# Three DMAs of 112, 8 and 8 partitions in place of one of 128, in the tail of a row sum

## The chip, the cores and the metric

The kernel runs on one core of one Trainium2 chip. The metric is the device time of one execution in microseconds (us). Before the change the median of three runs is 160.55 us (160.5 to 160.6). The profile is of a further execution, which took 160.47 us.

## What is computed

Each of 32 x 512 rows of 1024 float32 numbers is summed and the sum multiplied by 0.5.

```python
def setup_inputs():
    batch, seq, dim = 32, 512, 1024
    return {
        "x": np.random.randn(batch, seq, dim).astype(np.float32),
        "multiplier": 0.5,
    }

def reference(x: np.ndarray, multiplier: float) -> np.ndarray:
    return (np.sum(x, axis=-1) * multiplier).astype(np.float32)
```

## The kernel before

The 16384 rows are 128 for each of 128 partitions. One row per partition is the "head"; it is loaded first (L112), summed by ACT and turned into a form for its own small store by DVE (L113 to L119). The other 127 rows per partition are loaded in eight blocks: one of 15 rows, six of 16, and a last one of 16 that is loaded in five pieces. Three buffers (`xb`) of 16 rows go round. A row is 4 KB, so a block of 16 rows is 8 MB.

All DMAs are issued by SP, in the order of the program, and share one queue, whose transfers are served in order on the 16 DMA engines. The helper `load` (L79 to L88) allocates a semaphore, issues one `dma_start` (L82), which may wait first for a count of DVE's finished instructions (`free`, the buffer is free again) or for another load to land (`behind`), and adds 16 to the semaphore when all of it has landed. Whatever stands behind a waiting issue on SP waits too.

For the first six blocks DVE sums the whole block (L136) and scales the sums (L142). The seventh block is shared: DVE sums eight of its rows, ACT the other eight (`act_row`, L91). The last block comes in these pieces, which are named here for the rest of the text:

- p0: rows 0 to 9; p1: rows 10 to 13; p2: row 14 and the first 384 columns of row 15 (L163 to L173, sizes in `bounds`);
- e0: columns 384 to 735 of row 15, 352 columns, 1408 B per partition; e1: the last 288 columns (L174 to L182, sizes in `cuts`).

e0 and e1 go to a tensor `end` of their own. e0 is issued when the seventh block has landed (`behind`), e1 when DVE has summed its half of the seventh block (`free`).

In the last block ACT sums rows 1, 4, 7, 9, 13 and 14 and DVE the others, each as a sum of two halves with an accumulator (`dve_sum`, L101; in the profile a CUSTOM_DVE_ANT_0 and a READ_ACCUMULATOR). Row 15 is summed in three steps on DVE: the first 384 columns as 192 pairs (L205), e0's 352 columns as 176 pairs (L207, `second`), and e1's 288 columns together with the two partial sums, as 145 pairs (L210, `final`). `second` waits for e0 (L206). `final` waits for 17 on e1's semaphore: 16 of its landing and one that `second` adds (L209, L211).

There are three stores. The results of the first seven blocks go out after ACT's and DVE's parts of the seventh block (L184, "the early store"). The head's results follow in a DMA of four partitions of 128 B each (L188). The last store (L214) waits for 2 on `summed_up`: one from ACT after row 14 (L200) and one from `final` (L212). SP then waits for all stores.

Of the kernel before, what the change touches and what calls it, by code (L numbers as in the profile page):

```python
# [9 lines left out]
def kernel(  # L10
# [13 lines left out]
    nc = tc.nc  # L24
# [4 lines left out]
    P = nc.NUM_PARTITIONS  # L29
# [4 lines left out]
    N, D = x_flat.shape  # L34
# [4 lines left out]
    B = 16  # L39
    n_blocks = rows // B  # L40
# [5 lines left out]
    x_last = x_flat[P * own : N, :].rearrange("(p c) d -> p c d", p=P)  # L46
# [4 lines left out]
    def sbuf(name, *shape):  # L51
        return ctx.enter_context(nc.sbuf_tensor(name, list(shape), fp32)).ap()
# [8 lines left out]
    cuts = [384, 736, D]  # L61
    at = 368
    end = sbuf("end", P, at + D - cuts[1])

    def sem(name):
        return nc.alloc_semaphore(name=name)

    dve_done = sem("dve_done")
# [7 lines left out]
        counts[engine] += 1  # L76
        return counts[engine]

    def load(name, dst, src, free=None, behind=None):  # L79

        landed = sem(name)
        i = nc.sync.dma_start(out=dst, in_=src)  # L82
        if free is not None:
            i.wait_op(dve_done, free, "sem-ge")
        if behind is not None:
            i.wait_op(behind, 16, "sem-ge")
        i.then_inc(landed, 16)
        return landed  # L88

    def act_row(t, r, dst):  # L90
        return nc.scalar.activation(  # L91
            out=t[:, r, :],
            in_=t[:, r, :],
            func=mybir.ActivationFunctionType.Copy,
            scale=mul,
            accum_out=dst,
        )

    def dve_sum(row, dst, scale):
        mid = row.shape[-1] // 2  # L100
        return nc.vector.tensor_tensor_reduce(  # L101
            out=row[:, 0:mid],
            in0=row[:, 0:mid],
            in1=row[:, mid:],
            scale=scale,
            scalar=0.0,
            op0=ADD,
            op1=ADD,
            accum_out=dst,
        )  # L110

    landed_head = load("landed_head", head[:, 0, :], x_flat[0:P, :])  # L112
    cleared = marks(nc.vector.memset(column, 0.0), "dve")  # L113
    nc.scalar.wait_ge(landed_head, 16)
# [6 lines left out]
    freed = []  # L121
    blocks = []
    for b, n in enumerate(sizes):
        c0 = 1 + sum(sizes[:b])
        t = buf[b % bufs][:, 0:n, :]
        landed = load(
            f"landed{b}",
            t,
            x_rows[:, c0 - 1 : c0 - 1 + n, :],
            freed[b - bufs] if b >= bufs else None,  # L130
        )
# [5 lines left out]
                out=sums[:, c0 : c0 + h], in_=t[:, 0:h, :], axis=mybir.AxisListType.X  # L137
# [5 lines left out]
            out=res[:, c0 : c0 + h],  # L143
            in_=sums[:, c0 : c0 + h],
# [5 lines left out]
        if h < n:  # L150
            nc.scalar.wait_ge(landed, 16)
            for r in range(h, n):
                i = act_row(t, r, res[:, c0 + r : c0 + r + 1])
# [5 lines left out]
    flat = t.rearrange("p c d -> p (c d)")  # L159
    flat_last = x_last.rearrange("p c d -> p (c d)")  # L160
    bounds = [0, 10 * D, 14 * D, 15 * D + cuts[0]]

    landed = [  # L163
        load(f"landed_p{k}", flat[:, lo:hi], flat_last[:, lo:hi], free, behind)
        for k, (lo, hi, free, behind) in enumerate(
            zip(
                bounds[:-1],
                bounds[1:],
                (None, None, freed[n_blocks - 3]),
                (None, blocks[n_blocks - 3], None),  # L170
            )
        )
    ]  # L173
    landed_end = [  # L174
        load(f"landed_e{k}", end[:, to : to + hi - lo], x_last[:, B - 1, lo:hi], free, behind)
        for k, (to, lo, hi, free, behind) in enumerate(
            (
                (0, cuts[0], cuts[1], None, blocks[n_blocks - 2]),
                (at, cuts[1], D, freed[n_blocks - 2], None),
            )  # L180
        )
    ]  # L182
# [10 lines left out]
    on_act = {1, 4, 7, 9, 13, 14}  # L193
    for k, (lo, hi) in enumerate(((0, 10), (10, 14), (14, 15))):
        on = [r for r in range(lo, hi) if r in on_act]
        nc.scalar.wait_ge(landed[k], 16)
        for r in on:
            i = act_row(t, r, res[:, c0 + r : c0 + r + 1])
        if k == len(landed) - 1:
            i.then_inc(summed_up, 1)  # L200
        on = [r for r in range(lo, hi) if r not in on_act]
        nc.vector.wait_ge(landed[k], 16)
        for r in on:
            dve_sum(t[:, r, :], res[:, c0 + r : c0 + r + 1], mul)
    dve_sum(t[:, B - 1, 0 : cuts[0]], end[:, at - 2 : at - 1], 1.0)  # L205
    nc.vector.wait_ge(landed_end[0], 16)  # L206
    second = dve_sum(end[:, 0 : cuts[1] - cuts[0]], end[:, at - 1 : at], 1.0)  # L207

    second.then_inc(landed_end[1], 1)  # L209
# [75 lines left out]
```

## Time and profile before

| what | value |
|---|---|
| median of 3 runs | 160.55 us (160.5 to 160.6) |
| the profiled execution | 160.47 us |
| its span (first to last profiled event) | 159.2 us |
| DMA queue, share of 16 engines' span | 98.0% |
| HBM read | 67.11 MB, 422 GB/s over the span |
| e0: from issue to landing | 19.2 us |
| e1: from issue to landing | 10.8 us |
| last store: from issue to landing | 1.4 us |

The span is what the profile covers; 1.3 us of the execution's time lie around it. All times inside the execution are from the span's start. "To landing" is from the issue of a DMA on SP to the last increment of its semaphore; a DMA that is issued behind others in the queue spends most of this time waiting for them. The profile's page groups instructions by line, engine and shape; the timeline lists them in order of time, with the idle time before each in square brackets and what ended it. The trace also records every increment of a DMA's semaphore and every packet of a transfer, with its start, duration and size, but not which of the 16 DMA engines carried it.

### The profile page before, as it was taken

How to read it: one execution, taken by the hardware profiler on the slowest of the kernel's cores; microseconds unless marked ns; L12 is line 12 of the kernel's file. 1: busy time of each engine (PE TensorE's matmuls, PEld its weight loads, DVE VectorE, ACT ScalarE, POOL GpSimd, SP SyncE). 2: the span in 40 equal slices, each digit the busy share in tenths (PEclk: the TensorE clock that was granted, in tenths of full speed). 3: DMA queues.
4: the chain of work that ended last, by engine and by line, in shares of the span. 5: the costliest groups of instructions: out<-in, count | busy, mean ns of one | idle time of the engine just before them, and what ended most of it. 6: DMA issues, size and time to landing. Idle time of an engine off the chain costs nothing.

```text
span 159.2 us, 131 instructions
## 1 busy us (share of the span) xinstructions
DVE 119.1 (75%) x40; ACT 17.4 (11%) x31; POOL 0.2 (0%) x4
## 2 busy tenths in 40 slices
DVE  0000059995799968999599995999959999598376
ACT  2300000000000000000000000000000000397384
POOL 0000000000000000000000000000000000000000
DMA  9997996996997999969969969969989799798994
GB/s 379 494 401 340 494 527 264 527 527 264 527 461 329 527 395 395 527 280 511 527 264 527 527 264 527 494 296 527 445 346 527 346 445 527 329 453 371 420 401 151
DMA packets 2168, 67.18 MB, mean 422 GB/s; under 512 B 504, under 2 KB 760, under 8 KB 1016
## 3 DMA queue, kind: packets, MB, share of 16 engines
q1 hardware_dynamic: 2168, 67.18, 98.0%
HBM read 67.11 MB, written 0.07 MB: 422 GB/s over the span
## 4 chain that ended last, share of the span: by engine, by line
DMA 74%; DVE 24%; another core or an unknown queue 1%; SPq 1%; issue 0%
DMA xb<-in_x_dram 74%; DVE sums L136 22%; DVE xb L101 1%; SPq L82 1%; DVE end L101 0%; DVE res L142 0%; DVE res L101 0%
## 5 line engine op out<-in xcount | busy, mean ns | idle before, releaser
L136 DVE TENSOR_REDUCE sums<-xb 128x16 f32<-128x16384 f32 (+2 forms) x7 | 110.9, 15849 | 28.4 <-DMA xb<-in_x_dram 28.4
L91 ACT ACTIVATE xb<-xb 128x1024 f32<-128x1024 f32 x14 | 14.6, 1045 | 137.1 <-DMA xb<-in_x_dram 137.1
L101 DVE CUSTOM_DVE_ANT_0 xb<-xb 128x512 f32<-128x512 f32 (+1 forms) x10 | 5.9, 652 | 4.4 <-DMA xb<-in_x_dram 4.4
L91 ACT ACTIVATION_READ_ACCUMULATOR xb<-xb 128x1 f32 x14 | 2.6, 187 | 0.0
L113 DVE MEMSET column<- 128x32 f32 x1 | 0.1, 85 | 3.0 <-PEq L26 3.0
L117 DVE STREAM_TRANSPOSE row<-column 128x32 f32<-128x32 f32 x1 | 0.2, 212 | 2.6 <-ACT head L91 2.6
L91 ACT ACT_TABLE_LOAD x1 | 1.3, 1283 | 3.1 <-DVE column L113 3.1
L142 DVE TENSOR_SCALAR res<-sums 128x16 f32<-128x16 f32 (+2 forms) x7 | 1.2, 174 | 0.2
L91 ACT ACTIVATE head<-head 128x1024 f32<-128x1024 f32 x1 | 1.1, 1056 | 0.0
L101 DVE DVE_READ_ACCUMULATOR2_ANT res<- 128x1 f32 x10 | 0.8, 80 | 0.0
L101 DVE CUSTOM_DVE_ANT_0 end<-end 128x176 f32<-128x176 f32 (+1 forms) x2 | 0.7, 326 | 0.0
L91 ACT ACTIVATION_READ_ACCUMULATOR head<-head 128x1 f32 x1 | 0.2, 186 | 0.0
L101 DVE DVE_READ_ACCUMULATOR2_ANT end<- 128x1 f32 x2 | 0.2, 82 | 0.0
L266 POOL MEMSET const-bfloat16-1.0<- 128x1 bf16 x1 | 0.1, 101 | 0.0
L266 POOL MEMSET const-uint8-127<- 128x1 uint8 x1 | 0.1, 101 | 0.0
L266 POOL MEMSET const-float32-0.0<- 128x1 f32 x1 | 0.1, 98 | 0.2 <-issue 0.2
L266 POOL MEMSET const-float32-1.0<- 128x1 f32 x1 | 0.1, 98 | 0.0
## 6 DMA issues: line engine op xcount, KB each, us to landing
xb<-in_x_dram SPq DMA_DIRECT2D x1, 7680.0 KB, 21.2
xb<-in_x_dram SPq DMA_DIRECT2D x1, 5120.0 KB, 33.6
xb<-in_x_dram SPq DMA_DIRECT2D x1, 2048.0 KB, 36.4
xb<-in_x_dram SPq DMA_DIRECT2D x1, 704.0 KB, 20.8
head<-in_x_dram SPq DMA_DIRECT2D x1, 512.0 KB, 3.3
end<-in_x_dram SPq DMA_DIRECT2D x1, 176.0 KB, 19.2
end<-in_x_dram SPq DMA_DIRECT2D x1, 144.0 KB, 10.8
xb<-in_x_dram SPq DMA_DIRECT2D x6, 40.8
```

Source lines behind the costliest of these rows:

```text
L82: i = nc.sync.dma_start(out=dst, in_=src)
L91: return nc.scalar.activation(out=t[:, r, :], in_=t[:, r, :], func=mybir.ActivationFunctionType.Copy, scale=mul, accum_out=dst,)
L101: return nc.vector.tensor_tensor_reduce(out=row[:, 0:mid], in0=row[:, 0:mid], in1=row[:, mid:], scale=scale, scalar=0.0, op0=ADD, op1=ADD, ...
L113: cleared = marks(nc.vector.memset(column, 0.0), "dve")
L117: turned = nc.vector.transpose(out=row, in_=column)
L136: nc.vector.reduce_sum(out=sums[:, c0 : c0 + h], in_=t[:, 0:h, :], axis=mybir.AxisListType.X),
L142: scaled = nc.vector.tensor_single_scalar(out=res[:, c0 : c0 + h], in_=sums[:, c0 : c0 + h], scalar=mul, op=mybir.AluOpType.mult,)
L266: nc = _bacc.Bacc("TRN2", target_bir_lowering=False, num_devices=1)
```

## The change

`load` takes a list of partition counts and issues one DMA for each, all on the same semaphore; only the first one waits. The wait for e0 then asks for 16 times the number of DMAs. Only e0 gets more than one: 112, 8 and 8 partitions. The sums, the columns and the other loads stay as they are.

```diff
-    def load(name, dst, src, free=None, behind=None):
+    def load(name, dst, src, free=None, behind=None, groups=(P,)):
 
         landed = sem(name)
-        i = nc.sync.dma_start(out=dst, in_=src)
-        if free is not None:
-            i.wait_op(dve_done, free, "sem-ge")
-        if behind is not None:
-            i.wait_op(behind, 16, "sem-ge")
-        i.then_inc(landed, 16)
+        p0 = 0
+        for n in groups:
+            i = nc.sync.dma_start(out=dst[p0 : p0 + n], in_=src[p0 : p0 + n])
+            if free is not None and p0 == 0:
+                i.wait_op(dve_done, free, "sem-ge")
+            if behind is not None and p0 == 0:
+                i.wait_op(behind, 16, "sem-ge")
+            i.then_inc(landed, 16)
+            p0 += n
+        assert p0 == P
         return landed
...
+    groups_end = (112, 8, 8)
     landed_end = [
...
-                (0, cuts[0], cuts[1], None, blocks[n_blocks - 2]),
-                (at, cuts[1], D, freed[n_blocks - 2], None),
+                (0, cuts[0], cuts[1], None, blocks[n_blocks - 2], groups_end),
+                (at, cuts[1], D, freed[n_blocks - 2], None, (P,)),
...
-    nc.vector.wait_ge(landed_end[0], 16)
+    nc.vector.wait_ge(landed_end[0], 16 * len(groups_end))
```

More of the change, by code (lines that the diff above doesn't have):

```diff
@@ L161 @@
     bounds = [0, 10 * D, 14 * D, 15 * D + cuts[0]]
+    groups = ((P,), (P,), (P,))
     landed = [
-        load(f"landed_p{k}", flat[:, lo:hi], flat_last[:, lo:hi], free, behind)
-        for k, (lo, hi, free, behind) in enumerate(
+        load(f"landed_p{k}", flat[:, lo:hi], flat_last[:, lo:hi], free, behind, parts)
+        for k, (lo, hi, free, behind, parts) in enumerate(
             zip(
@@ L170 @@
                 (None, blocks[n_blocks - 3], None),
+                groups,
             )
@@ L173 @@
     ]
+    groups_end = (112, 8, 8)
     landed_end = [
-        load(f"landed_e{k}", end[:, to : to + hi - lo], x_last[:, B - 1, lo:hi], free, behind)
-        for k, (to, lo, hi, free, behind) in enumerate(
-            (
-                (0, cuts[0], cuts[1], None, blocks[n_blocks - 2]),
-                (at, cuts[1], D, freed[n_blocks - 2], None),
+        load(
+            f"landed_e{k}",
+            end[:, to : to + hi - lo],
+            x_last[:, B - 1, lo:hi],
+            free,
+            behind,
+            parts,
+        )
+        for k, (to, lo, hi, free, behind, parts) in enumerate(
+            (
+                (0, cuts[0], cuts[1], None, blocks[n_blocks - 2], groups_end),
+                (at, cuts[1], D, freed[n_blocks - 2], None, (P,)),
             )
@@ L195 @@
         on = [r for r in range(lo, hi) if r in on_act]
-        nc.scalar.wait_ge(landed[k], 16)
+        nc.scalar.wait_ge(landed[k], 16 * len(groups[k]))
         for r in on:
@@ L201 @@
         on = [r for r in range(lo, hi) if r not in on_act]
-        nc.vector.wait_ge(landed[k], 16)
+        nc.vector.wait_ge(landed[k], 16 * len(groups[k]))
         for r in on:
```

## The prediction

> **What bounds the kernel now.** I read the page from the top: the span, the shares of the engines, then the chain that ended last.
>
> ```profile
> span 159.2 us, 131 instructions
> ...
> DVE 119.1 (75%) x40; ACT 17.4 (11%) x31; POOL 0.2 (0%) x4
> ...
> q1 hardware_dynamic: 2168, 67.18, 98.0%
> ...
> DMA 74%; DVE 24%; another core or an unknown queue 1%; SPq 1%; issue 0%
> DMA xb<-in_x_dram 74%; DVE sums L136 22%; DVE xb L101 1%; SPq L82 1%; DVE end L101 0%; DVE res L142 0%; DVE res L101 0%
> ```
>
> The one DMA queue is busy for 98% of 16 engines' span: the 67 MB bound the kernel, and the diff moves the same bytes. What can change is the tail behind the last large load. So next I read the timeline of the last three microseconds (start, duration, instruction, and the wait before it).
>
> ```profile
> 156.50 1.06 ACT L91 ACTIVATE xb<-xb 128x1024 f32<-128x1024 f32 x1 [0.58 <-DMA xb<-in_x_dram]
> 156.62 0.08 DVE L101 DVE_READ_ACCUMULATOR2_ANT res<- 128x1 f32 x1
> 156.62 0.35 DVE L101 CUSTOM_DVE_ANT_0 xb<-xb 128x192 f32<-128x192 f32 x1
> 156.89 0.08 DVE L101 DVE_READ_ACCUMULATOR2_ANT end<- 128x1 f32 x1
> 156.97 0.34 DVE L101 CUSTOM_DVE_ANT_0 end<-end 128x176 f32<-128x176 f32 x1
> 157.24 0.08 DVE L101 DVE_READ_ACCUMULATOR2_ANT end<- 128x1 f32 x1
> 157.36 0.31 DVE L101 CUSTOM_DVE_ANT_0 end<-end 128x145 f32<-128x145 f32 x1
> 157.47 0.19 ACT L91 ACTIVATION_READ_ACCUMULATOR xb<-xb 128x1 f32 x1
> 157.59 0.08 DVE L101 DVE_READ_ACCUMULATOR2_ANT res<- 128x1 f32 x1
> 157.70 0.34 SPq L214 DMA_DIRECT2D out_dram<-res  x1
> ```
>
> Two things are to be seen. First, each sum starts together with the READ_ACCUMULATOR of the one before it (156.62 and 156.62); only the sum over the 176 pairs, which reads the changed load, starts 0.08 us after its predecessor's (156.89, 156.97). The chain of waits shows no idle time there, because the 0.08 us are filled by the READ_ACCUMULATOR. The semaphore's record in the trace gives the reason: the changed load (e0 below) reaches 16 at 156.949, and a wait on a landing ends 0.023 to 0.024 us later elsewhere (154.748 to 154.771, 149.855 to 149.879); 156.949 + 0.024 = 156.973. So **e0's last landing is on the path, by 0.079 us** (156.973 - 156.894).
>
> Second, the final store waits for two increments. DVE's comes at 157.688, ACT's, after its last row (156.50 + 1.06 + the accumulator), at 157.661. ACT is only **0.027 us** behind being the bound.
>
> **What the change does, part by part.** *The rows.* e0 is 128 rows of 1408 B, eight to a DMA engine. The packet records show 16 chains of eight rows in steps of 57 ns (from 155.583 to 155.983 is seven steps), then a semaphore packet, then the next DMA's rows. The 16 landings fall in two halves: eight from 156.487 to 156.628, eight from 156.676 to 156.949, and the same two halves stand in the earlier loads. 112 rows on 16 engines are seven each; eight rows on eight engines are one each. So eight engines get 7 rows, the other eight 7 + 1 + 1 = 9.
>
> Which half gets nine? The trace doesn't name a packet's engine, but one DMA in it is smaller than 16: the four-row store of L188. Its semaphore has one landing record at issue and four later ones, so it ran on four engines, and its four packets (starting 156.608, 156.680, 156.681, 156.701) each begin 6 ns after a semaphore packet of four of the early chains. So small DMAs go to engines of the early half; I take the eight early ones for eight rows, an extension of this row.
>
> Then the late half ends one row sooner: 156.949 - 0.057 = 156.892. The early half ends one row and two semaphore packets (6 ns of a chain each at most) later: 156.628 + 0.057 + 0.012 = 156.697. The last landing is 156.892 and the second sum may start at 156.916 in place of 156.973: **-0.057 us**. DVE itself would be ready at 156.894, so no larger gain is there to be had.
>
> *The next load (e1, 288 columns)* stands behind e0 in every chain: its last landing goes from 157.310 to 157.253, while the final sum waits for the second's increment (157.335, moving to 157.278). It follows the second by 0.024, so DVE's last increment is at 157.688 - 0.057 = 157.631.
>
> *The store.* Now ACT's 157.661 is last. Its row came with the load before e0 in every chain (landed 156.479, started 156.503), which the change doesn't touch. The store goes out 0.016 us behind the later increment: 157.677 in place of 157.704. **Of 0.057 us, 0.027 remain.** From the store to the end of the span are 1.45 us as before.
>
> *SP's issues.* Two DMAs more. An ordinary issue takes 328 ns, the four-row store 635 ns, so 0.7 to 1.3 us. They follow e0's release at 137.75, and the next instruction, e1's issue, waits for DVE until 146.47: over 7 us of cover. e0's first packet starts at 155.58, 17 us after. Without this cover, e1, the early store and the four-row store would go out that much later. Cost here: nothing. The wait count (48 in place of 16) is still one wait, with the second and the final sum queued behind it on DVE.
>
> *The landing of small groups.* The trace has no 8-row load. From below: nothing beyond the row steps above, since the next DMA's rows follow a semaphore packet within 6 ns. From above: rows of one group that meet at one place in SBUF could queue; that is a rival, with both ends there. I take the lower end, as the 16 chains ran at an even 57 ns next to each other.
>
> [...]
>
> *Sum.* -0.027 us against the profiled execution's 160.47 (span 159.2 and 1.3 around it) gives 160.44. The median of the three runs, 160.55, is 0.08 above that execution, so the forecast is 160.55 - 0.03 = **160.52 us**. A measurement of this kernel can tell about 0.2% (0.32 us) from no change, so this is "the same".
>
> **Rivals.**
>
> 1. *The small groups' rows queue at SBUF* (ends slower). In the 128-row load every engine fills its own partitions; in a group of eight, eight engines write neighbouring partitions at the same time. A row's bytes take 52 ns (65536 B take 2418 ns). If n of the eight wait for each other, each group costs the early half up to (n - 1) x 0.052 us more. It has 0.321 us of slack (156.949 - 156.628), of which 0.069 are used, so from n = 4 on it decides: e0 lands at 156.697 + 6 x 0.052 = 157.009, or +0.060 us; n = 8 gives 157.425, or +0.476. Times: **160.61 to 161.03**. The group of 112, whose sevens no longer match the old eights, could add row waits of the same kind: seven at most, 0.364 us. For it: partitions are now shared. Against: nothing in the trace shows such a wait. [...]
> 2. *An eight-row group runs on one engine.* Sixteen rows on it in place of one: 15 x 0.057 = 0.86 us on an early chain, 156.487 or 156.628 + 0.86, so e0 lands 0.4 to 0.54 us later: **160.95 to 161.1**. Against: the four-row store ran on four engines.
> 3. *The eight engines are the late ones.* 156.949 + 0.069: +0.07 us, **160.62**. Against: the four-row store's chains.
> 4. *Each group waits for the one before to land.* From the last row's end (156.501) to the landing are 0.448 us; twice that on the early half gives 156.628 + 0.90 = 157.53, +0.58: **161.1**. [...]
> 5. *e0's landing isn't the gate*, or the split doesn't shift it: **160.55**, which no measurement tells from the forecast and goes with it.
>
> **How the numbers follow.** Forecast (with 5) 0.50. Rival 1: 0.33, of which 0.09 lies beyond +0.32 us (n of 7 or 8, or waits in the large group too). Rival 2: 0.05, beyond. Rival 3: 0.05, within 0.2%. Rival 4: 0.03, beyond. Something that no row shows, faster by over 0.2%: 0.04; the cap by ACT speaks against any such gain. Same: 0.50 + 0.24 + 0.05 = 0.79. Slower: 0.09 + 0.05 + 0.03 = 0.17. Faster: 0.04. The range goes from 160.40 (the forecast less the 0.1 us over which the three runs scatter) to 161.00, which takes in rival 1 but its last step and leaves out most of 2 and 4, about 1 in 10.
>
> **What would show it.** Right: the eight latest landings of e0 lie about 0.06 us nearer to those of the load before it, the 176-pair sum starts 0.02 rather than 0.08 us behind its READ_ACCUMULATOR, and the store starts 0.016 us behind ACT's increment. Rival 1: packets of 1408 B in the small groups that take longer than 60 ns, and the early half landing last. Rival 2: one chain with sixteen rows. Rival 3: the late half landing 0.07 later. Rival 4: gaps of 0.4 us in the chains. The prediction is wrong if the loads before e0 land at other times, since nothing in the diff reaches them.

## The result, and the profile after

The changed kernel takes 160.84 us (median of 22 runs, 160.73 to 161.12), the kernel before 160.53 us beside it (22 runs, 160.44 to 160.76). The ratio is 1.002 with a 95% interval of 1.0013 to 1.0026: slower by 0.31 us, where 0.03 us less was forecast. The time lies inside the stated range, but on the other side of the kernel before, and the rows moved off an engine bring nothing that can be seen. The interval excludes a kernel that takes the same time, though the difference is no more than the 0.2% that the prediction gave as the least that a measurement can tell.

The profiled execution of the changed kernel took 160.92 us. From its page: the span, DVE's share, the queue, and the chain that ended last.

```profile
span 159.6 us, 133 instructions
...
DVE 119.2 (75%) x40; ACT 17.4 (11%) x31; POOL 0.2 (0%) x4
...
q1 hardware_dynamic: 2184, 67.18, 98.0%
...
DMA 77%; DVE 21%; SPq 1%; issue 0%
DMA xb<-in_x_dram 65%; DVE sums L140 21%; DMA end<-in_x_dram 12%; SPq L84 1%; DVE end L105 0%; DVE res L105 0%
```

The bytes and DVE's work are the same. The chain is new: the load of `end`, e0, stands in it by name with 12%, where before the chain went through DVE. (L84, L105 and L140 are L82, L101 and L136 of the kernel before.) The timeline of its tail:

```profile
156.95 1.06 ACT L95 ACTIVATE xb<-xb 128x1024 f32<-128x1024 f32 x1 [0.96 <-DMA xb<-in_x_dram]
156.95 0.36 DVE L105 CUSTOM_DVE_ANT_0 xb<-xb 128x192 f32<-128x192 f32 x1 [0.19 <-DMA xb<-in_x_dram]
157.23 0.08 DVE L105 DVE_READ_ACCUMULATOR2_ANT end<- 128x1 f32 x1
157.42 0.34 DVE L105 CUSTOM_DVE_ANT_0 end<-end 128x176 f32<-128x176 f32 x1
157.69 0.08 DVE L105 DVE_READ_ACCUMULATOR2_ANT end<- 128x1 f32 x1
157.81 0.31 DVE L105 CUSTOM_DVE_ANT_0 end<-end 128x145 f32<-128x145 f32 x1
157.91 0.19 ACT L95 ACTIVATION_READ_ACCUMULATOR xb<-xb 128x1 f32 x1
158.04 0.08 DVE L105 DVE_READ_ACCUMULATOR2_ANT res<- 128x1 f32 x1
158.15 0.34 SPq L228 DMA_DIRECT2D out_dram<-res  x1
```

The 176-pair sum starts 0.19 us after its predecessor's READ_ACCUMULATOR (157.23 to 157.42); it was 0.08. The semaphore's record has e0's last landing at 157.397, 0.023 us before. e0's last packet had ended at 156.651, so the landing came 0.75 us behind it; before, 0.45 (156.501 to 156.949). Counted from the end of p1's last packet, which nothing in the change reaches (154.362; before, 154.318), e0's last packet ended 0.11 us later than before and its last landing came 0.40 later. Also p2, which stands ahead of e0 in the queue, landed late: 156.923, 2.11 us after p1 in place of 1.73, and both DVE and ACT wait for it.

The packet records show what became of the even steps. Before, 127 of e0's 128 packets of 1408 B took 60 to 65 ns and all of e1's 128 of 1152 B took 51. After, e0's took up to 108 ns, 35 of them over 65, and 87 of e1's over 56, although e1 itself was not touched. In the tail it is e0's landing that counts: in every profile of this document the 176-pair sum starts 0.02 to 0.03 us behind it, and the final sum 0.38 to 0.39 us after that, while e1's last landing lies 0.04 us or more ahead of the final sum. So e1's slow packets are a sign of what goes on and no cost of their own.

### The profile page after: what moved, and what is told of

The parts are those of the page before. It is cut to its first block, busy times and chain, and to the rows that moved or that the text cites. A ratio compares the mean times of both kernels' runs of the same rounds, so it can differ in the third digit from the quotient of the medians.

```text
span 159.6 us, 133 instructions
## 1 busy us (share of the span) xinstructions
DVE 119.2 (75%) x40; ACT 17.4 (11%) x31; POOL 0.2 (0%) x4
## 4 chain that ended last, share of the span: by engine, by line
DMA 77%; DVE 21%; SPq 1%; issue 0%
DMA xb<-in_x_dram 65%; DVE sums L140 21%; DMA end<-in_x_dram 12%; SPq L84 1%; DVE end L105 0%; DVE res L105 0%
## 5 line engine op out<-in xcount | busy, mean ns | idle before, releaser
L140 DVE TENSOR_REDUCE sums<-xb 128x16 f32<-128x16384 f32 (+2 forms) x7 | 110.9, 15849 | 28.5 <-DMA xb<-in_x_dram 28.5
L105 DVE CUSTOM_DVE_ANT_0 xb<-xb 128x512 f32<-128x512 f32 (+1 forms) x10 | 6.0, 654 | 4.5 <-DMA xb<-in_x_dram 4.5
L105 DVE DVE_READ_ACCUMULATOR2_ANT res<- 128x1 f32 x10 | 0.8, 82 | 0.0
L105 DVE CUSTOM_DVE_ANT_0 end<-end 128x176 f32<-128x176 f32 (+1 forms) x2 | 0.7, 327 | 0.1
L105 DVE DVE_READ_ACCUMULATOR2_ANT end<- 128x1 f32 x2 | 0.2, 82 | 0.0
```

Source lines behind the costliest of these rows:

```text
L105: return nc.vector.tensor_tensor_reduce(out=row[:, 0:mid], in0=row[:, 0:mid], in1=row[:, mid:], scale=scale, scalar=0.0, op0=ADD, op1=ADD, ...
L140: nc.vector.reduce_sum(out=sums[:, c0 : c0 + h], in_=t[:, 0:h, :], axis=mybir.AxisListType.X),
```

## The experiments

Three theories stood for the +0.31 us. *Shared places*: in a load of 128 partitions each engine fills its own eight; in a group of 112, or 8, an engine writes to partitions that lie where another engine is still writing, and the rows wait. In the kernel before e0's 128 packets start in steps of 57 ns and land in 16 increments, which the prediction reads as 16 chains of eight; which eight partitions a chain fills no trace shows, as none names a packet's engine. That they are the same in every load is part of the theory. *Small groups*: the two groups of eight cost it, with nine rows on eight engines. *Count*: each further DMA on the semaphore costs something by itself. A fourth came up on the way: *crowded landings*.

All times are medians beside the kernel before, measured with it. Each edit is shown against the changed kernel, unless another is named. "Excess" is what the packets of 1408 B took over 60 ns, and those of 1152 B over 51 ns, summed over all engines. "Delay" is how far the k-th landing lies behind the k-th semaphore packet, as a median over p2, e0, e1 and the two earlier stores of one profile. The last column has the end of e0's last packet and e0's last landing, both counted from the end of p1's last packet.

| run | time, before (us) | ratio, 95% interval | excess 1408 B, 1152 B (us) | delay (us) | e0's last packet, landing (us) |
|---|---|---|---|---|---|
| before | | | 0.04, 0.00 | 0.47 | 2.18, 2.63 |
| after | 160.84, 160.53 | 1.002 [1.0013, 1.0026] | 0.85, 1.50 | 0.68 | 2.29, 3.04 |
| g112_16 | 160.97, 160.53 | 1.0029 [1.0018, 1.0041] | 0.09, 0.52 | 0.62 | 2.46, 3.15 |
| two_column_parts | 160.63, 160.53 | 1.0005 [0.9997, 1.0014] | (704 B: 0.00), 0.19 | 0.49 | 2.28, 2.74 |
| whole_and_two_eights | 160.90, 160.53 | 1.002 [1.001, 1.003] | 0.12, 1.73 | 0.62 | 2.25, 2.89 |
| g64_64 | 160.96, 160.53 | 1.0033 [1.0021, 1.0046] | 2.03, 3.02 | 0.71 | 2.50, 3.20 |
| two_eights_own_places | 160.70, 160.56 | 1.0008 [1.0, 1.0017] | 0.04, 0.00 | 0.60 | 2.18, 2.89 |
| source_shifted | 160.57, 160.56 | 1.0 [0.9991, 1.0009] | 0.01, 0.00 | 0.48 | 2.43, 2.83 |
| p0_112_16 | 173.06, 160.56 | 1.0776 [1.0759, 1.0792] | (40960 B, see below) | | 2.18, 2.66 |
| before_again | 160.48 (one) | | 0.02, 0.00 | 0.48 | 2.18, 2.61 |
| two_tiny_eights | 160.68, 160.53 | 1.0009 [1.0, 1.0017] | 0.01, 0.00 | 0.60 | 2.16, 2.77 |
| g112_eights_own_places | 160.90, 160.53 | 1.0023 [1.0013, 1.0033] | 0.71, 1.65 | 0.65 | 2.24, 2.95 |
| after_again | 161.09 (one) | | 1.10, 2.17 | 0.69 | 2.31, 3.26 |
| two_tiny_eights_early | 160.56, 160.55 | 0.9998 [0.9989, 1.0008] | 0.02, 0.00 | 0.48 | 2.16, 2.64 |

### First four: which part of the change

```diff
-    groups_end = (112, 8, 8)
+    groups_end = (112, 16)
```

> Three theories for the +0.31 us of the change. Shared places: in the 128-partition load each DMA engine writes its own eight partitions; in a group of 112 an engine's seven rows lie in partitions that other engines are still filling, and the rows wait for each other. Small groups: the two groups of eight, nine rows on eight of the engines, cost it. Count: each further DMA on the semaphore costs something by itself. Here 352 columns go as 112 and 16 partitions, eight rows on every engine, two DMAs. Shared places: still slower, +0.2 to +0.4 us, with packets of 1408 B well over 60 ns. Small groups: 0.00 to +0.05 us. Count: about half of the change's, +0.15 us, with packets at 60 ns.

+0.44 us, with eight rows on each engine and no group of eight. Small groups as the sole cause fall, and so does half of the change for half of its further DMAs. The excess is smaller than expected, 0.6 us in sum, though the time is longer; in this profile p2's packets, ahead of e0's, also stall (see before_again below) and end 0.27 us later, so how its 0.44 us divide is not settled.

```diff
+        w = dst.shape[-1] * P // sum(groups)
...
-            i = nc.sync.dma_start(out=dst[p0 : p0 + n], in_=src[p0 : p0 + n])
+            c = p0 // P * w
+            to, of = (dst, src) if len(groups) == 1 else (dst[:, c : c + w], src[:, c : c + w])
+            i = nc.sync.dma_start(out=to, in_=of)
...
-    groups_end = (112, 8, 8)
+    groups_end = (P, P)
```

> The 352 columns go as two DMAs of 128 partitions and 176 columns each on one semaphore, so every engine keeps its own partitions. Rows of 704 B should take about 34 ns (26 for the bytes, 8 more for each row), sixteen on an engine in place of eight of 60. Shared places: packets at 34 ns with no spread, the landing later by 16 x 34 - 8 x 60 = 0.06 us and the time +0.06 us at most. Small groups: the same. Count: +0.15 us or more, with the landing later by more than its packets explain.

+0.10 us, with an interval that holds both no change and +0.22. The 256 packets of 704 B took 34 ns, none over 35. Two DMAs of all 128 partitions cost 0.22 us at most. The run has as many DMAs and landings as g112_16 before it and g64_64 below, which cost 0.44 and 0.43 us, with intervals that lie wholly above its own: splitting by partitions costs some 0.33 us more than splitting by columns.

```diff
+    spare = sbuf("spare", P, cuts[1] - cuts[0])
...
-            i = nc.sync.dma_start(out=dst[p0 : p0 + n], in_=src[p0 : p0 + n])
+            to, q = (dst, p0) if p0 < P else (spare, p0 - 16)
+            i = nc.sync.dma_start(out=to[q : q + n], in_=src[q : q + n])
...
-    groups_end = (112, 8, 8)
+    groups_end = (P, 8, 8)
```

> The 352 columns go as one DMA of 128 partitions, and the last 16 partitions' rows are loaded a second time, as two DMAs of eight, to a spare tensor, on the same semaphore, which is waited for at 48. Added against before: the two small groups alone, two rows of 57 ns on eight engines. If those are the early eight, 0.32 us of slack cover the 0.11 us. Small groups: the full +0.3 us or more. Shared places: less than the change, 0 to +0.2 us, since only 16 rows lie in foreign partitions; packets of 1408 B over 60 ns are few. Count: +0.3 us.

+0.37 us, more than shared places gave it. The two groups of eight, added to a whole load, cost as much as the change. Only 3 of the 144 packets of 1408 B took over 65 ns; of e1's, 51 of 128 took over 56 ns, up to 112. Sixteen further rows, written to partitions 112 to 127, disturb the load behind them.

```diff
-    groups_end = (112, 8, 8)
+    groups_end = (64, 64)
```

> The 352 columns go as two DMAs of 64 partitions, four rows on every engine each. [...] Small groups: 0.00 to +0.05 us. Count: +0.15 us, packets at 60 ns.

+0.43 us, and the largest excess of all, 5 us in sum, with packets of 1408 B up to 174 ns. It has neither a group of eight nor an engine with more rows than another.

### Next four: is it the place?

Against whole_and_two_eights, with the sixteen spare rows in other partitions. That they meet no other engine's rows there was the author's assumption; no trace shows which engine fills a partition:

```diff
-            to, q = (dst, p0) if p0 < P else (spare, p0 - 16)
-            i = nc.sync.dma_start(out=to[q : q + n], in_=src[q : q + n])
+            q, own_q = (p0, p0) if p0 < P else (p0 - 16, 4 * (p0 - P))
+            to = dst if p0 < P else spare[own_q : own_q + 4 * n : 4]
+            i = nc.sync.dma_start(out=to, in_=src[q : q + n])
```

> As whole_and_two_eights (one DMA of 128 partitions, then 16 rows loaded again in two DMAs of eight, +0.37 us), but the spare rows go to partitions 0, 4, ..., 28 and 32, 36, ..., 60 in place of 112 to 127. [...] DMAs, rows, bytes, semaphore and SP's work are the same. Shared places: most of the +0.37 us goes, to between 0.00 and +0.12 us (two rows of 57 ns on eight engines), and the 1152 B packets of the next load are back at 51 ns (an excess of 1.7 us over all of them before). Small groups or the count of DMAs: +0.37 us as it was.

Of +0.37 us, +0.14 are left, and e1's packets are back at 51 ns, all 128. Nothing but the partitions of sixteen spare rows differs between the two programs (SP takes 1.4 us in place of 0.7 to issue these two DMAs, some 17 us before their rows move). The two times' intervals overlap a little; the excess of e1's packets, 1.73 us against 0.00, does not leave the same doubt. But the two profiles don't show where the 0.2 us between the medians arise: e0 lands 2.89 us after p1's last packet in both, and the 0.13 us between the two profiled executions lie ahead of that packet's end (154.443 and 154.306). The +0.14 is just above what was expected (0.12), and the timeline shows where it sits:

```profile
156.60 0.35 DVE L108 CUSTOM_DVE_ANT_0 xb<-xb 128x192 f32<-128x192 f32 x1
156.88 0.08 DVE L108 DVE_READ_ACCUMULATOR2_ANT end<- 128x1 f32 x1
157.22 0.34 DVE L108 CUSTOM_DVE_ANT_0 end<-end 128x176 f32<-128x176 f32 x1 [0.26 <-DMA spare<-in_x_dram]
157.46 0.19 ACT L98 ACTIVATION_READ_ACCUMULATOR xb<-xb 128x1 f32 x1
157.49 0.08 DVE L108 DVE_READ_ACCUMULATOR2_ANT end<- 128x1 f32 x1
157.61 0.31 DVE L108 CUSTOM_DVE_ANT_0 end<-end 128x145 f32<-128x145 f32 x1
```

DVE waits idle for 0.26 us for the last of 32 landings (157.198), while the last packet of 1408 B had ended at 156.490: 0.71 us behind. Between 156.723 and 157.018 the record has 22 landings of e0, all but one step 13 or 14 ns apart. This is a cost of its own, and the last experiments follow it.

Against the kernel before:

```diff
+    x_prev = x_flat[P * own - 4 * B : N - 4 * B, :].rearrange("(p c) d -> p c d", p=P)
...
-        load(f"landed_e{k}", end[:, to : to + hi - lo], x_last[:, B - 1, lo:hi], free, behind)
+        load(f"landed_e{k}", end[:, to : to + hi - lo], (x_prev if k == 0 else x_last)[:, B - 1, lo:hi], free, behind)
```

> The kernel before, with the 352 columns in one DMA of 128 partitions, but read from rows that lie four partitions earlier in HBM (so row 15 of the last block gets other numbers in these columns). [...] Shared places in SBUF: as before, within 0.05 us, packets at 60 ns. A rival theory, that the engines meet at the source in HBM and not in SBUF: +0.1 us or more, packets over 60 ns.

No change (+0.01 us), e0's packets at 60 to 64 and e1's at 51 ns. Reading from rows four partitions earlier does nothing; writing the spare rows to other partitions took the excess of e1's packets from 1.73 us to 0.00 (whole_and_two_eights, two_eights_own_places).

```diff
-    groups = ((P,), (P,), (P,))
+    groups = ((112, 16), (P,), (P,))
...
-    groups_end = (112, 8, 8)
+    groups_end = (P,)
```

> The 352 columns are one DMA of 128 again; instead the first piece of the last block (ten rows, 40960 B per partition, packets of 1514 ns) goes as 112 and 16 partitions. Shared places: the waits grow with the rows, which are 25 times as long: g112_16 cost 0.44 us, so several us, +4 to +11 us, with packets well over 1514 ns. A fixed price for each DMA, each small group or each semaphore: +0.5 us at most.

+12.5 us, more than the upper end, where g112_16 with rows of 1408 B cost 0.44: the cost is larger with the longer rows. The stretches of this run (DVE busy, ACT busy, POOL busy, clock, DMA share, GB/s) show how it looks:

```profile
137.00:155.00 18.00, 8.86 (x2) 8.43 (x16) 0.00 (x0) 1.00 1.08 262
155.00:163.00 8.00, 0.48 (x1) 0.48 (x1) 0.00 (x0) 1.00 0.81 156
```

and the same stage of the kernel before:

```profile
137.75:149.88 12.13, 8.86 (x3) 8.43 (x17) 0.00 (x0) 1.00 0.96 415
```

In the first stretch the engines count as busy all the time (a share of 1.08, so packets overlap), and in the second for 81% of it, but they move 262 and then 156 GB/s in place of 415: their packets take longer for the same bytes. A packet of 40960 B took 1.51 us before. Here the 112 rows took 1.96 to 2.98, 2.74 in the median, about 1.8 times as long, and the 16 rows of the second group 4.4 to 5.4, up to 3.6 times. The load's last packet ends at 161.452 in place of 149.437, 12.0 us later. Why the second group's rows take the longest is not shown. Behind it DVE waits for p0 and p1, 16.2 us in two waits, the longest of 15.3 (before, 4.4 in two):

```profile
DVE xb L105 <- DMA xb<-in_x_dram: 16.2, 2, 15.3
```

The kernel before once more, unchanged:

> The kernel before once more, for a second profile. In the profile after, packets of the load before the changed one took up to 387 ns in place of 215 from 154.25 to 155.3 us, ahead of any changed packet (155.585). If that stall comes with some executions whatever the kernel, it can show here too; the 1408 B and 1152 B packets stand at 60 and 51 ns whether it does or not. If the change makes it, the 5632 B packets stay under 225 ns here.

This second profile of the kernel before has no stall: one packet of 5632 B took 253 ns, the others under 240. But source_shifted, which costs nothing and has no groups, has it: 5632 B packets up to 418 ns from 154.5 to 155.4. So have two_column_parts (up to 405) and g112_16 (up to 398). The stall comes with some executions; in the first profile after it began at 154.25, ahead of e0's first packet. What it is was not tried. In that profile p2's last packet ended 1.77 us after p1's, against 1.72 in the two profiles before, so the stall moved p2's end by 0.05 us; after_again has the later landing of e0 without it (below). In source_shifted it moved e0's last packet by 0.24 us, and that execution took 0.08 us more than its median. How often it comes in executions without a profile is not known.

### Last four: what is left besides places

Against two_eights_own_places:

```diff
+            of = src[q : q + n]
+            if p0 >= P:
+                to, of = to[:, 0:4], of[:, 0:4]
-            i = nc.sync.dma_start(out=to, in_=src[q : q + n])
+            i = nc.sync.dma_start(out=to, in_=of)
```

> As two_eights_own_places (+0.14 us), but the two extra DMAs of eight rows load 4 columns (16 B) in place of 352. What is left of +0.14 us? There, the changed load's 32 landings and the next 16 came up to 0.73 us behind their packets (about 0.47 before), as if landings were taken one at a time, some 13 ns each. Landings theory: 16 more landings in the same stretch cost as before, +0.08 to +0.15 us, and landings come over 0.55 us (median) behind their packets. Rows theory: only the extra rows cost; two rows of about 9 ns leave +0.00 to +0.03 us and the median delay stays at 0.47 to 0.49.

+0.15 us with sixteen rows of 9 ns. The rows don't cost it, the landings do: delay 0.60 us, e0's last landing at 157.136 though its last packet ended at 156.526, 0.61 us before (0.45 in the kernel before). Other DMAs' landings come later too: e1's first at 157.052, before at 156.854. But the number of landings is not all: two_column_parts has just as many, and there the delay is 0.49 us and e0 lands 0.46 us behind its last packet. Its 32 landings are spread over 0.91 us, here they fall within 0.61.

As the change, but its two groups of eight go to the spare partitions of two_eights_own_places; partitions 112 to 127 of the tile hold zeros from a memset at the start, so the 352 columns of these rows are left out of the sums:

```diff
+    spare = sbuf("spare", P, cuts[1] - cuts[0])
...
-            i = nc.sync.dma_start(out=dst[p0 : p0 + n], in_=src[p0 : p0 + n])
+            to = dst[p0 : p0 + n]
+            if n == 8:
+                to = spare[4 * (p0 - 112) : 4 * (p0 - 112) + 4 * n : 4]
+            i = nc.sync.dma_start(out=to, in_=src[p0 : p0 + n])
...
+    nc.vector.memset(end[96:P, 0 : cuts[1] - cuts[0]], 0.0)
```

> [...] Bytes, DMAs and landings are those of the change (+0.31 us). Shared places: the 112 rows still meet, 1408 B packets over 60 ns, +0.15 to +0.35 us. Rival, that only the eights' neighbouring partitions meet: packets at 60 and 51 ns and +0.0 to +0.14 us, as with two_eights_own_places.

+0.37 us, just above what was expected, with packets of 1408 B up to 100 ns. The group of 112 costs time by itself: with a whole load in its place (two_eights_own_places), the same two eights cost 0.14 us. The eights' other places make no difference to the change that can be told, so the parts don't add up.

The changed kernel once more, unchanged:

> The changed kernel once more, for a second profile. Shared places: 1408 B and 1152 B packets again with an excess of one to two us in sum over 60 and 51 ns. The stall of 5632 B packets at 154 to 155 us may or may not be there; it was there with source_shifted, which costs nothing. If it is not, the end shows what the shared places and the landings cost without it: the store some 0.2 to 0.35 us later against the load two before (before: 2.96 us after p1's last landing).

The excess is there again and larger than expected (3.3 us in sum), without the stall (5632 B packets under 232 ns). The store goes out 3.57 us after p1's last landing in place of 2.96, 0.6 us later where 0.2 to 0.35 was expected. Its tail, from the timeline:

```profile
156.64 0.08 DVE L105 DVE_READ_ACCUMULATOR2_ANT res<- 128x1 f32 x1
156.84 1.06 ACT L95 ACTIVATE xb<-xb 128x1024 f32<-128x1024 f32 x1 [0.89 <-DMA xb<-in_x_dram]
156.84 0.36 DVE L105 CUSTOM_DVE_ANT_0 xb<-xb 128x192 f32<-128x192 f32 x1
157.12 0.08 DVE L105 DVE_READ_ACCUMULATOR2_ANT end<- 128x1 f32 x1
157.61 0.34 DVE L105 CUSTOM_DVE_ANT_0 end<-end 128x176 f32<-128x176 f32 x1 [0.40 <-DMA end<-in_x_dram]
```

p2's landing is late here too (156.817), by 2.04 us after p1's against 1.73, though its packets were not slow: its last landings stand among e0's. This goes with where the rows are written, not with the landings' number: counted from p1's last packet, p2 has landed at 2.16 us before, at 2.16 and 2.15 in two_eights_own_places and two_tiny_eights, at 2.32 in whole_and_two_eights, 2.34 in g112_eights_own_places and 2.50 here. The 176-pair sum then waits another 0.40 us. This execution took 161.09 us, 0.25 above the median of the changed kernel.

Against two_tiny_eights:

```diff
-    groups = ((P,), (P,), (P,))
+    groups = ((P, 8, 8), (P,), (P,))
...
-    groups_end = (P, 8, 8)
+    groups_end = (P,)
```

> As two_tiny_eights (+0.15 us), but the two tiny DMAs of eight rows go with the first piece of the last block, on its semaphore (waited for at 48), some 7 us before the end, where only this piece's 16 landings come. Crowded landings: nothing queues there that the end needs, so 0.00 to +0.04 us, and landings in the tail are 0.47 to 0.49 us (median) behind their packets again. A price for each further DMA or landing wherever it comes: +0.15 us again.

The same two DMAs and 16 landings cost no time here (0.9998), and the delay in the tail is 0.48 again. In the tail they cost 0.15. But p0's landings are delayed here as e0's were there: 0.56 us in the median, against 0.41 in two_tiny_eights, and the last one comes 0.49 us behind p0's last packet, against 0.38. The time doesn't show it because DVE then waits 1.04 us for p1, and ACT 0.54, in place of 1.13 and 0.62. So this run doesn't tell a crowd of landings from a price for each further DMA; it shows that either is free on a load whose landing is not the one that the end waits for. That in two_tiny_eights e1's first landing comes later too, on another semaphore, speaks for landings that hold each other up; this is argued and not shown.

```profile
150.02 1.06 ACT L101 ACTIVATE xb<-xb 128x1024 f32<-128x1024 f32 x1 [3.79 <-DMA spare<-in_x_dram]
150.02 0.69 DVE L111 CUSTOM_DVE_ANT_0 xb<-xb 128x512 f32<-128x512 f32 x1 [3.33 <-DMA spare<-in_x_dram]
...
154.82 1.06 ACT L101 ACTIVATE xb<-xb 128x1024 f32<-128x1024 f32 x1 [0.54 <-DMA xb<-in_x_dram]
154.82 0.69 DVE L111 CUSTOM_DVE_ANT_0 xb<-xb 128x512 f32<-128x512 f32 x1 [1.04 <-DMA xb<-in_x_dram]
```

In the tail the 176-pair sum starts as in the kernel before, 0.09 us behind its predecessor's READ_ACCUMULATOR:

```profile
156.94 0.08 DVE L111 DVE_READ_ACCUMULATOR2_ANT end<- 128x1 f32 x1
157.03 0.34 DVE L111 CUSTOM_DVE_ANT_0 end<-end 128x176 f32<-128x176 f32 x1
```

## Why the prediction failed, point by point

**What bounds the tail** was right. e0's landing gates the 176-pair sum: before_again shows it too (landing 156.958, sum at 156.982, DVE ready at 156.923). After the change this is where the time comes in.

**The step that failed** is "The landing of small groups", with "nothing beyond the row steps above". The lower end was taken because the 16 chains ran at an even 57 ns beside each other. They did so in the 128-partition load, and the change splits it: a load split by partitions is slower than one split by columns (+0.44 us in g112_16 and +0.43 in g64_64 against +0.10 in two_column_parts), and e1's packets are slow or not by the places of sixteen spare rows (an excess of 1.73 us in whole_and_two_eights, 0.00 in two_eights_own_places). The even steps were no evidence for a split load. After the change packets of 1408 B took up to 108 ns, and e0's last landing, counted from p1's last packet, came 0.40 us later (0.63 in after_again), where 0.06 less was forecast. It failed twice:

- *Places.* Rival 1 came nearest, with 0.33: rows that take longer for where they are written; its 160.61 to 161.03 holds the time. It put the place in the two small groups and made the large one an addition; with the eights in other places the kernel with the large one still takes 0.37 us more, where the same eights behind a whole load take 0.14 more. It also took e0's rows to meet each other only, while e1's rows lost the most (1.50 of 2.35 us of excess), though nothing waits for that. That its bounds hold the time is in part luck, as the landings below are no part of it. No run shows rival 1's n, the number of rows that wait for each other, nor that they wait in SBUF; the runs show packets of 1408 B of up to 108 ns after the change and up to 174 in g64_64, in place of 60.
- *Landings.* Their number was counted as nothing ("still one wait"). Two groups of eight on 16 more landings, with next to no bytes, cost 0.15 us on the load that the end waits for, and none on p0, where idle time takes the same delay up. The prediction moved e0's last landing with its last row, as if the 0.45 us between them were fixed; it was 0.61 in two_tiny_eights. In the kernel before 52 landings of e0, e1 and the two earlier stores fall in 1.07 us (156.487 to 157.555), 21 ns each; 16 more in the same time make 16 ns, close to the 13 ns below which e0's never fall in any profile. That they then wait for each other is an argument from these numbers. No run here times one write of a semaphore by itself; with 16 more of them in the tail the landings come 0.60 us behind their packets in place of 0.47.

**That the change doesn't touch p2**, the load before e0 in every chain, was wrong: its packets are untouched in after_again, its last landing is not (156.817, where 156.479 was taken as fixed). With it the start of ACT's last row moves. The prediction had named this, loads before e0 that land at other times, as a sign of being wrong.

**The gain of a row** on the late engines (-0.057 us, of which ACT would leave 0.027) can't be seen under these costs, and no run shows it by itself. That g112_16 with eight rows everywhere was 0.13 us slower than the change would fit it, but their intervals overlap.

**The slack of the early half** (0.321 us) rests on a reading that was weak from the start: the step between the two halves is 48 ns, while steps of 94 and 95 ns lie inside the late one. In before_again p1's landings are spread from 154.244 to 154.777 and e0's from 156.432 to 156.958, with no two halves.

**SP's cover** held: the three issues of e0 took 1.1 us from 137.81, and e1's issue stood at 146.53. **Rivals 2 and 4** are out: e0's semaphore has 32 landings besides two records at issue, so, read as the four-row store was, each group of eight ran on eight engines; and no two of e0's packets start more than 0.1 us after one another. Rival 3 (which half the eight are) was not settled.

That splitting by partitions costs time is shown at equal DMAs and landings (+0.44 and +0.43 us against +0.10 for two_column_parts). How the change's own +0.31 us divides stays open: two further groups of eight in the places of two_eights_own_places cost 0.14 and 0.15 (two runs, each with an interval from 0.00 to 0.27), the places the rest, but the parts don't add up, and both delay the same landing. No version here beats the kernel before.

## What to carry to other kernels

Before a full-width load is split by partitions, ask what its even packet time rests on: here 1408 B took 60 to 65 ns in all but one packet of the whole load and up to 108 ns in the split one. A row less on the late engines was estimated at 0.057 us; splitting by partitions cost a multiple, and more with longer rows (112 and 16 partitions: 0.44 us for 1408 B, 12.5 us for 40960 B). Two further DMAs of eight rows were free on a load behind whose landing the engines idle anyway (a ratio of 0.9998, with DVE idle for 1.04 us after it), and cost some 0.15 us on the load that the end waits for, so look at how the landings of the last microsecond come as well as at the bytes. And a packet that takes longer is not yet lost time: e1's lost the most in the changed kernel (1.50 of 2.35 us), and nothing waited for them.

## What the runs showed of the hardware that was not expected

- Landings came later behind their packets with 16 more of them on the same load: 0.47 us in the kernel before and 0.60 in two_tiny_eights in the tail, 0.41 in two_tiny_eights and 0.56 in two_tiny_eights_early for p0; with 16 more that were spread wider (two_column_parts) 0.49 in the tail. e1's, on another semaphore, are later as well: its first came at 157.127 in two_eights_own_places and 157.052 in two_tiny_eights, while before it was 156.854. In every profile e0's increments are at least 13 ns apart, e1's 11, p0's 5, so no one price of a landing can be read from them.
- Rows of a load took 1.3 to 3.6 times as long (p0_112_16, 40960 B: 1.96 to 5.42 us in place of 1.51) for the choice of partitions in each DMA alone.
- The DMA engines were "busy" by their share and moved little in p0_112_16: 1.08 with 262 GB/s, against 0.96 with 415 in the kernel before.
- Four of the profiles have a stall of 0.8 to 1.0 us in the loads from 154.25 to 154.5 us on, with packets up to 1.9 times as long, with and without a split load.
